# A gated linear recurrence inside a two-layer hybrid decoder: its chunks worked out as a scan

## The chip, the core and the metric

The kernel runs on one core of one Trainium2 chip. TensorE (PE) multiplies, VectorE (DVE) and ScalarE (ACT) do elementwise work and empty PSUM, GpSimd (POOL) does some elementwise work, SyncE (SP) issues most DMAs. The metric is the device time of one execution in microseconds, a median of several runs. Everything is fp32; large products are split into three fp32r products of a high and a low part.

## The reference

A trunk of two layers over 512 tokens of width 1024. Each layer is a feed-forward block, four mixers side by side on a common projection, an output projection, and a second feed-forward block. The change is in one mixer, RWKV-7, with four heads of 64 channels and a 64x64 state S for each head:

```
sa = S @ kk_t
S  = S * w_t - sa (x) (kk_t*a_t) + v_t (x) k_t
y  = S @ r_t
```

It is computed in 8 chunks of 64 tokens; afterwards y is normalized for each head, a bonus is added and a gate multiplied. Another mixer that shares the same stretch of time is NSA, attention with compressed, selected and windowed keys.

## The kernel before

For each mixer pass, 21 projection tiles (tilep, 24 PE products of 512 columns each) make the inputs. Rwkv.prep makes for each head pair j the chunk operands KR (keys kk and queries r, scaled by the running decay), AK (the two kinds of written keys) and W (the chunk's total decay), and puts the transposed v into sav. Rwkv.solve then makes M, the masked products of AK and KR inside each chunk (L1010, masked on DVE at L1012), sends its key part through DRAM (adram) into another layout, inverts 16x16 blocks by forward substitution on DVE (L1030, L1032), sends the result back through DRAM (tdram), and joins the blocks on PE to 64x64 inverses T64 (L1057 to L1088). Last it scales AK by W and transposes it (L1093 to L1097).

Rwkv.chain goes through the chunks in series. For each one: right side from the state H and from v (L898, L901, accumulated in PSUM), copied to R (L904), multiplied by T64 (L910), copied into sav beside v (L911, L912), multiplied by AK (L920), and added to the decayed state (L928 for chunk 0, else four updates at L931). H is kept as five rotating tiles with the two heads of a pair on the diagonal of a 128x128 block. Rwkv.out(g) makes the outputs of four chunks (L948 from the state, L951 from sav), normalizes them (ln, L983 to L995), transposes (L959), gates (L969 to L971) and puts them.

The order of instructions is made ahead of time from priorities: an instruction with a lower number goes first once its operands and buffers are there. Projection tiles 0 to 12 come first. Then solve stands at p0, chain and out at p0 + 300 (chunks 0 to 3) and p0 + 500 (chunks 4 to 7), attention's 16 units at p0 + 2000, and as filler at p0 + 3000 the remaining projection tiles, pool and convolution, with the pool's product at L810. Within an engine the order then is fixed, and an instruction that waits holds up all behind it. PSUM: solve and out take tiles from net.pr (tag "r", two buffers), chain from tag "c" (one). The ring "s" (line 466) has seven SBUF buffers for attention scores, their transposes and the compression weights.

The output projection (order 0, 1, 6, 7, 4, 5, 2, 3 over the mixers' tiles) needs all mixers; 4 and 5 are attention's, 2 and 3 the recurrence's.

Of the kernel before, what the change touches and what calls it, by code (L numbers as in the profile page):

```python
# [26 lines left out]
HD = 64  # L27
C = 64
NC = S // C
# [69 lines left out]
class Net:  # L99
# [290 lines left out]
    def mixers(self, tilep, cmpk, cmpv):  # L390
        nc = self.nc
# [39 lines left out]
        rw = st["rw"]  # L431
# [13 lines left out]
        def chain(g):  # L445
            for _ in rw.chain(g):
                pass
            rw.out(g)
# [17 lines left out]
    def ring(self):  # L466
        return self.mt("s", [P, S], bufs=7)

    def rring(self):
        return self.mt("s", [P, S], F32R, bufs=7)  # L470
# [343 lines left out]
class Rwkv:  # L814
    def __init__(self, net, sh):
        self.net, self.sh = net, sh
        nc = net.nc
        self.T0 = sh["L0"]
        nc.scalar.activation(self.T0, self.T0, AF.Tanh, scale=net.c["sc"])
        nc.vector.tensor_scalar(self.T0[64:], self.T0[64:], 0.5, 0.5, ALU.mult, ALU.add)  # L820
        self.sav = net.mt("sav", [P, NC, 2, 2, HD])
        self.KR, self.AK, self.W, self.bv = [], [], [], []
        self.Hb = []
        for i in range(5):
            h = net.mt(f"H{i}", [P, 2, P])
            nc.gpsimd.memset(h, 0.0)
            self.Hb.append(h)
# [58 lines left out]

    def chain(self, g):
        net = self.net
        nc, sav, KR, W = net.nc, self.sav, self.KR, self.W
        M, T64 = self.M, self.T64  # L890
        for cc in range(4):
            ch = 4 * g + cc
            H = self.Hb[ch % 5]
            pr = net.psum("c", 1)
            for j in range(2):
                a, b = slice(64 * j, 64 * j + 64), slice(64 * (1 - j), 64 * (2 - j))
                if ch > 0:
                    nc.tensor.matmul(pr[a, 0:P], KR[j][:, ch, 0], H[:, j], start=True, stop=False)  # L898
                for hp in range(2):
                    o = pr[a, hp * 64:hp * 64 + 64]  # L900
                    nc.tensor.matmul(o, M[b, j, hp, ch, 0], sav[b, ch, j, hp], start=(ch == 0),  # L901
                                     stop=(ch == 0 or hp == 1))
            R = net.mt("R", [P, P], bufs=2)
            nc.scalar.copy(R, pr[:, :P])  # L904
            pa = net.psum("c", 1)
            for j in range(2):
                a = slice(64 * j, 64 * j + 64)
                for hp in range(2):
                    hs = slice(64 * hp, 64 * hp + 64)
                    nc.tensor.matmul(pa[a, hs], T64[a, hp, ch], R[a, hs], start=True, stop=True)  # L910
            nc.scalar.copy(sav[0:64, ch, 0].rearrange("p b d -> p (b d)"), pa[0:64, :P])  # L911
            nc.vector.tensor_copy(sav[64:, ch, 1].rearrange("p b d -> p (b d)"), pa[64:, :P])  # L912
            if ch == NC - 1:
                yield
                return
            phs = net.psum("c", 1)
            for j in range(2):
                for hp in range(2):
                    hs = slice(64 * hp, 64 * hp + 64)
                    nc.tensor.matmul(phs[hs, j * 64:j * 64 + 64],  # L920
                                     self.AK[j][:, ch].rearrange("p a b -> p (a b)")[:, hs], sav[:, ch, j, hp],
                                     start=True, stop=True)
            Hn = self.Hb[(ch + 1) % 5]
            for hp in range(2):
                hs = slice(64 * hp, 64 * hp + 64)
                p3 = phs[hs, 0:P].rearrange("p (j v) -> p j v", v=HD)
                if ch == 0:
                    nc.vector.tensor_copy(Hn[hs, :, hs], p3)  # L928
                else:
                    for j in range(2):  # L930
                        nc.vector.scalar_tensor_tensor(Hn[hs, j, hs], H[hs, j, hs], W[j][hs, ch:ch + 1],  # L931
                                                       p3[:, j], ALU.mult, ALU.add)
            yield

    def out(self, g):
        net = self.net
        nc, v, sav, KR = net.nc, net.v, self.sav, self.KR
        M = self.M
        py = []
        for j in range(2):  # L940
            p = net.pr()[:, 0:256]
            p4 = p.rearrange("p (c h v) -> p c h v", c=2, h=2)
            for cc in range(4):
                ch = 4 * g + cc
                H = self.Hb[ch % 5]
                par = slice(64 * (ch % 2), 64 * (ch % 2) + 64)
                if ch > 0:
                    nc.tensor.matmul(p4[par, cc // 2].rearrange("p h v -> p (h v)"), KR[j][:, ch, 1], H[:, j],  # L948
                                     start=True, stop=False)
                for hp in range(2):  # L950
                    nc.tensor.matmul(p4[par, cc // 2, hp], M[:, j, hp, ch, 1], sav[:, ch, j, hp], start=(ch == 0),  # L951
                                     stop=(ch == 0 or hp == 1))
# [22 lines left out]
    def ln(self, py):  # L975
        net = self.net
        nc = net.nc
        bc = lambda a: a.unsqueeze(2).to_broadcast([P, 4, HD])
        y = net.tmp()[:, :S].rearrange("p (j c h v) -> p j c h v", j=2, c=2, h=2)
        yf = y.rearrange("p j c h v -> p j (c h) v")  # L980
        mu = net.small(8, "lmu")
        for j in range(2):
            nc.vector.tensor_reduce(mu[:, 4 * j:4 * j + 4], py[j].rearrange("p (a v) -> p a v", v=HD), AX.X, ALU.add)  # L983
        nc.vector.tensor_scalar(mu, mu, 1.0 / HD, None, ALU.mult)
        for j in range(2):
            nc.vector.tensor_sub(yf[:, j], py[j].rearrange("p (a v) -> p a v", v=HD), bc(mu[:, 4 * j:4 * j + 4]))
# [11 lines left out]
    def solve(self):  # L998
        net = self.net
# [20 lines left out]
        dma(blk, ad[:, 0:1024].rearrange("b (i t) -> b i t", t=C)[:, :, 0:16])  # L1020
        Tb = net.tmp()[:, :S].rearrange("p (k a b) -> p k a b", k=2, a=16)
# [67 lines left out]
        for g in range(2):  # L1089
            for j in range(2):  # L1090
                ake = net.tmp()[:, :S].rearrange("p (a b) -> p a b", b=P)
                akv = AK[j][:, 4 * g:4 * g + 4].rearrange("p c a b -> p c (a b)")
                nc.vector.tensor_mul(ake, akv, W[j][:, 4 * g:4 * g + 4].unsqueeze(2).to_broadcast([P, 4, P]))  # L1093
                pk = net.pr()
                for cc in range(4):
                    nc.tensor.transpose(pk[:, cc * P:(cc + 1) * P], ake[:, cc], net.ident)
                nc.scalar.copy(akv, pk.rearrange("p (c a) -> p c a", c=4))  # L1097
        self.M, self.T64 = M, TT

# [125 lines left out]
```

## Time and profile before

| | us |
|---|---|
| median of 3 runs (2081.02 to 2084.48) | 2081.34 |
| the profiled execution | 2080.37 |
| its span, first to last instruction | 2078.6 |
| PE busy | 2026.1 |
| DVE busy | 1042.8 |
| ACT busy | 665.3 |
| POOL busy | 329.9 |

The span is that of the device's instructions; the run's time has 1.8 us around it. Busy times of PE overlap at their ends, as matmuls are pipelined, so the durations of PE's rows can't be added: what an instruction takes of PE's time is read from the start of one row to the start of the next. A row with xN stands for N instructions in series, and each fp32 product counts as two. The two mixing passes lie at about 380 to 660 us and 1410 to 1690 us; the feed-forward blocks, which fill the rest, are PE products without a gap.

### The profile page before, as it was taken

What the parts mean: (1) busy time and instruction counts of PE and PEld (TensorE: products, weight loads), DVE (VectorE), ACT (ScalarE), POOL (GpSimd) and SP (SyncE); (2) the same over time, 40 slices, a digit from 0 to 9 for tenths busy, and PEclk for the clock granted to TensorE, in tenths of its full rate; (3) what the DMA queues carried; (4) which work ended last, traced back from release to release, by engine and by line L of the source; (5) the groups of instructions that cost most, each with busy time, mean ns of one, the idle gap of its engine ahead of it and who ended that gap; (6) DMA issues with size and microseconds to landing.
All of it is one profiled execution on the core that took longest, in us unless ns stands there. A gap on an engine that the chain in (4) does not pass through costs nothing.

```text
span 2078.6 us, 25265 instructions
## 1 busy us (share of the span) xinstructions
PE 2026.1 (97%) x10132; PEld 1646.0 (79%) x10132; DVE 1042.8 (50%) x1866; ACT 665.3 (32%) x1053; POOL 329.9 (16%) x311
## 2 busy tenths in 40 slices
PE   8999999998999999999999999999988999999999
PEld 6888888876767888888888888887766778888887
DVE  5434344567676534343544343355686754334433
ACT  4322223332344322232333222233324443222221
POOL 1110111102332110011011001111033411100110
PEclk9999999998999999999999999999999999999999
DMA  5223223322302322322332232244133032223223
GB/s 198 93 90 103 101 89 124 128 102 64 71 18 91 102 89 82 114 90 89 104 102 102 84 110 100 75 133 149 68 74 77 1 102 102 95 84 116 86 92 97
DMA packets 61078, 196.76 MB, mean 95 GB/s; under 512 B 29472, under 2 KB 29600, under 8 KB 46240
## 3 DMA queue, kind: packets, MB, share of 16 engines
q1 hardware_dynamic: 58400, 186.76, 28.0%
q0 software_dynamic: 2560, 8.39, 1.1%
q8 instruction: 79, 1.29, 0.3%
q14 instruction: 39, 0.32, 0.0%
HBM read 183.58 MB, written 8.93 MB: 93 GB/s over the span
## 4 chain that ended last, share of the span: by engine, by line
PE 92%; DVE 4%; DMA 1%; issue 1%; ACT 1%; POOL 0%; SPq 0%; DVEq 0%; POOLq 0%; ACTq 0%
PE d L209 15%; PE d L210 15%; PE d L211 15%; PE r L211 8%; PE r L209 8%; PE r L210 8%; PE n L209 5%; PE n L211 5%; PE n L210 5%; PE o L623 1%; PE r L1010 1%; PE n L616 1%; PE d L589 0%; PE c L901 0%; DVE t L1032 0%
## 5 line engine op out<-in xcount | busy, mean ns | idle before, releaser
L203 ACT CAST wh<-w 128x1024 fp32r<-128x1024 f32 (+2 forms) x360 | 344.4, 957 | 1103.9 <-issue 334.5
L204 DVE TENSOR_TENSOR wl<-w,wh 128x1024 fp32r<-128x1024 f32 (+2 forms) x360 | 404.4, 1124 | 211.7 <-ACT wh L203 204.1
L209 PE MATMUL d<-hh,wh 128*128 128x512 f32 x1008 | 400.0, 397 | 6.8 <-ACT hh L216 6.8
L210 PE MATMUL d<-hl,wh 128*128 128x512 f32 x1008 | 400.6, 397 | 1.7 <-DVE hl L217 1.7
L211 PE MATMUL d<-hh,wl 128*128 128x512 f32 x1008 | 399.0, 396 | 0.0
L270 POOL TENSOR_TENSOR al<-t,ah 128x512 fp32r<-128x512 f32 x88 | 152.7, 1735 | 1062.5 <-ACT ah L269 1062.5
L210 PE MATMUL r<-hl,wh 128*128 128x512 f32 x736 | 286.8, 390 | 0.0
L211 PE MATMUL r<-hh,wl 128*128 128x512 f32 x736 | 286.5, 389 | 0.0
L209 PE MATMUL r<-hh,wh 128*128 128x512 f32 x736 | 286.5, 389 | 0.0
L209 PEld LDWEIGHTS d<-hh,wh 128*128 128x128 f32 x1008 | 192.6, 191 | 50.2 <-ACT hh L216 6.8
L210 PEld LDWEIGHTS d<-hl,wh 128*128 128x128 f32 x1008 | 192.4, 191 | 44.7 <-DVE hl L217 3.6
L211 PEld LDWEIGHTS d<-hh,wl 128*128 128x128 f32 x1008 | 192.4, 191 | 42.9 <-issue 2.0
L264 DVE TENSOR_TENSOR t<-d,rs 128x512 f32<-128x512 f32 x88 | 60.5, 691 | 266.3 <-PE d L211 260.5
L268 DVE TENSOR_TENSOR t<-t,r 128x512 f32<-128x512 f32 x88 | 60.5, 688 | 221.1 <-PE r L211 220.9
L209 PEld LDWEIGHTS r<-hh,wh 128*128 128x128 f32 x736 | 138.2, 188 | 28.7
L211 PEld LDWEIGHTS r<-hh,wl 128*128 128x128 f32 x736 | 138.2, 188 | 28.6
L210 PEld LDWEIGHTS r<-hl,wh 128*128 128x128 f32 x736 | 138.2, 188 | 28.5
L209 PE MATMUL d<-ah,wh 128*128 128x512 f32 x352 | 136.9, 389 | 0.0
L210 PE MATMUL d<-al,wh 128*128 128x512 f32 x352 | 136.9, 389 | 0.0
L211 PE MATMUL d<-ah,wl 128*128 128x512 f32 x352 | 136.9, 389 | 0.0
L209 PE MATMUL n<-ah,wh 128*128 128x512 f32 x352 | 136.9, 389 | 0.0
L210 PE MATMUL n<-al,wh 128*128 128x512 f32 x352 | 136.9, 389 | 0.0
(307 smaller groups left out, 2372.1 us busy)
## 6 DMA issues: line engine op xcount, KB each, us to landing
w<-in_g SPq DMA_DIRECT2D x87, 1024.0 KB, 4.9
w<-in_d SPq DMA_DIRECT2D x64, 704.0 KB, 4.1
w<-in_win SPq DMA_DIRECT2D x20, 1024.0 KB, 4.9
w<-in_wout SPq DMA_DIRECT2D x8, 1024.0 KB, 5.3
xd<-x POOLq DMA_DIRECT2D x16, 256.0 KB, 4.2
x<-xd POOLq DMA_DIRECT2D x16, 256.0 KB, 5.7
x<-in_x SPq DMA_DIRECT2D x8, 256.0 KB, 5.3
s<-in_cmpk SPq DMA_DIRECT2D x8, 256.0 KB, 5.9
```

What stands on the lines that cost most here:

```text
L203: self.nc.scalar.copy(hi, w)
L204: self.nc.vector.tensor_sub(lo, w, hi.bitcast(F32))
L209: self.nc.tensor.matmul(ps, wh[:, sl], xh[:, k], start=(first and i == 0), stop=False)
L210: self.nc.tensor.matmul(ps, wh[:, sl], xl[:, k], start=False, stop=False)
L211: self.nc.tensor.matmul(ps, wl[:, sl], xh[:, k], start=False, stop=(last and i == n - 1))
L264: nc.vector.tensor_mul(t, pg, self.rs)
L268: nc.vector.tensor_mul(th, th, pu)
L270: nc.gpsimd.tensor_sub(al, th, ah.bitcast(F32))
L616: nc.tensor.transpose(ptr[:, k * P:(k + 1) * P], scs[hp][:, b * P:(b + 1) * P], self.ident)
L623: nc.tensor.matmul(acc, VT[:, br, b], pT[k][:, o:o + 2 * P], start=(br == 0 and b == 0 and k == 0), stop=(br == 1 and b == i and k == 1))
L1010: nc.tensor.matmul(pm[:, i * P:(i + 1) * P], AK[j][hs, ch].rearrange("p a b -> p (a b)"), KR[j][hs, ch].rearrange("p a b -> p (a b)"), sta ...
```

## The change

The serial part of the recurrence is reduced to one product and one addition for each chunk. With G = T64 times the transposed keys, a chunk maps the state as H' = W*H + (AK^T G) H + AK^T u, where u = T64 M v needs no state. All G and u are worked out for all chunks together (carry, called at the end of solve), and from them the transition matrices (put into KR's key part) and the effective queries (added to KR's query part, as r + M G). What doesn't need the inverses (the transposed keys KT, the products of M and v, the scaled and transposed AK) is worked out in early, called in solve between the sending of M to DRAM and the forward substitution. out then takes the state against the effective queries, with K of 64 for each head in place of the block diagonal of 128; ln follows the new layout. The five H tiles (and their memsets) become one, and the ring "s" goes from seven buffers to six.

```diff
-        return self.mt("s", [P, S], bufs=7)
+        return self.mt("s", [P, S], bufs=6)
 ...
+    def early(self, M):
 ...
+        for g in range(2):
+            pk, pm = net.pr(), net.pr()
+            for j in range(2):
+                a, b = slice(64 * j, 64 * j + 64), slice(64 * (1 - j), 64 * (2 - j))
+                for cc in range(4):
+                    ch = 4 * g + cc
+                    nc.tensor.matmul(pk[a, cc * P:(cc + 1) * P], KR[j][:, ch, 0], net.ident, start=True, stop=True)
+                    for hp in range(2):
+                        o = cc * P + hp * HD
+                        nc.tensor.matmul(pm[a, o:o + HD], M[b, j, hp, ch, 0], sav[b, ch, j, hp], start=True, stop=True)
+            nc.scalar.copy(self.KT[:, 4 * g:4 * g + 4].rearrange("p c h k -> p (c h k)"), pk)
+            self.take(g, pm)
 ...
+    def carry(self):
 ...
+        for g in range(2):
+            pg, pu = net.pr(), net.pr()
+            for j, cc, hp, ch, a in each(g):
+                o = cc * P + hp * HD
+                nc.tensor.matmul(pg[a, o:o + HD], T64[a, hp, ch], self.KT[a, ch, hp], start=True, stop=True)
+            for j, cc, hp, ch, a in each(g):
+                o = cc * P + hp * HD
+                nc.tensor.matmul(pu[a, o:o + HD], T64[a, hp, ch], sav[a, ch, j, hp], start=True, stop=True)
+            for j, copy in enumerate((nc.scalar.copy, nc.vector.tensor_copy)):
+                a = slice(64 * j, 64 * j + 64)
+                copy(M[a, j, :, 4 * g:4 * g + 4, 0], pg[a].rearrange("p (c h k) -> p h c k", c=4, h=2))
+            self.take(g, pu)
+        for g in range(2):
+            pp = [net.pr(), net.pr()]
+            for j, cc, hp, ch, a in each(g):
+                hs, o = slice(64 * hp, 64 * hp + 64), cc * HD
+                nc.tensor.matmul(pp[j][hs, o:o + HD], M[a, j, hp, ch, 0],
+                                 AK[j][a, ch].rearrange("p a b -> p (a b)")[:, hs], start=True, stop=True)
+            for j, cc, hp, ch, a in each(g):
+                hs, o = slice(64 * hp, 64 * hp + 64), 256 + cc * HD
+                nc.tensor.matmul(pp[j][hs, o:o + HD], M[a, j, hp, ch, 0], M[a, j, hp, ch, 1], start=True, stop=True)
+            for j in range(2):
 ...
+                nc.scalar.copy(KR[j][:, cs, 0], part(0))
+                nc.vector.tensor_add(KR[j][:, cs, 1], KR[j][:, cs, 1], part(256))
 ...
     def chain(self, g):
+        for ch in range(4 * g, min(4 * g + 4, NC - 1)):
+            p = net.psum("c", 1)
             for j in range(2):
+                o = slice(j * HD, j * HD + HD)
                 for hp in range(2):
                     hs = slice(64 * hp, 64 * hp + 64)
+                    nc.tensor.matmul(p[hs, o], AK[j][:, ch].rearrange("p a b -> p (a b)")[:, hs], sav[:, ch, j, hp],
+                                     start=True, stop=(ch == 0))
+                if ch > 0:
+                    for hp in range(2):
+                        hs = slice(64 * hp, 64 * hp + 64)
+                        nc.tensor.matmul(p[hs, o], KR[j][hs, ch, 0], H[hs, ch, j], start=False, stop=True)
+            if ch == 0:
+                nc.vector.tensor_copy(H[:, 1].rearrange("p j v -> p (j v)"), p[:, 0:P])
+            else:
+                for j in range(2):
+                    nc.vector.scalar_tensor_tensor(H[:, ch + 1, j], H[:, ch, j], W[j][:, ch:ch + 1],
+                                                   p[:, j * HD:j * HD + HD], ALU.mult, ALU.add)
 
     def out(self, g):
 ...
+        for hp in range(2):
+            hs = slice(64 * hp, 64 * hp + 64)
+            p = net.pr()[:, 0:256].rearrange("p (j c v) -> p j c v", j=2, c=2)
+            for j in range(2):
+                for cc in range(4):
+                    ch = 4 * g + cc
+                    o = p[64 * (ch % 2):64 * (ch % 2) + 64, j, cc // 2]
+                    nc.tensor.matmul(o, M[:, j, hp, ch, 1], sav[:, ch, j, hp], start=True, stop=(ch == 0))
+                    if ch > 0:
+                        nc.tensor.matmul(o, KR[j][hs, ch, 1], self.H[hs, ch, j], start=False, stop=True)
             py.append(p)
 ...
     def solve(self):
 ...
         dma(blk, ad[:, 0:1024].rearrange("b (i t) -> b i t", t=C)[:, :, 0:16])
+        self.early(M)
         Tb = net.tmp()[:, :S].rearrange("p (k a b) -> p k a b", k=2, a=16)
 ...
-        for g in range(2):
-            for j in range(2):
-                ake = net.tmp()[:, :S].rearrange("p (a b) -> p a b", b=P)
 ...
         self.M, self.T64 = M, TT
+        self.carry()
```

early also holds the loop over AK that stood at the end of solve, and take copies one half of a PSUM tile into sav on ACT and the other on DVE.

## Rows read from the trace of the kernel before

**Rows 1.** the page, busy time of TensorE and the chain that ended last
```profile
PE 2026.1 (97%) x10132; PEld 1646.0 (79%) x10132; DVE 1042.8 (50%) x1866; ACT 665.3 (32%) x1053; POOL 329.9 (16%) x311
...
PE 92%; DVE 4%; DMA 1%; issue 1%; ACT 1%; POOL 0%; SPq 0%; DVEq 0%; POOLq 0%; ACTq 0%
```

**Rows 2.** busy time by stage, layer 0: PE, PEld, DVE, ACT, POOL, then PEclk
```profile
480.00:505.00 25.00, 25.00 (x154) 20.18 (x153) 19.47 (x36) 9.09 (x15) 3.44 (x7) 1.00 0.43 122
505.00:515.00 10.00, 2.61 (x6) 1.11 (x5) 8.93 (x20) 1.22 (x2) 6.81 (x7) 0.71 0.13 13
515.00:545.00 30.00, 28.03 (x222) 22.15 (x220) 19.64 (x60) 7.70 (x19) 11.83 (x12) 0.87 0.53 114
...
631.00:660.00 29.00, 25.19 (x122) 19.43 (x121) 17.89 (x46) 13.03 (x26) 7.51 (x10) 1.00 0.37 120
sum 180.00, PE 160.52 PEld 123.24 DVE 127.63 ACT 72.45 POOL 58.94; mean PE 20.07 PEld 15.40 DVE 15.95 ACT 9.06 POOL 7.37
```

**Rows 3.** the same table for the mixing pass of layer 1, its sum
```profile
sum 180.00, PE 160.27 PEld 122.35 DVE 130.54 ACT 73.44 POOL 60.92; mean PE 20.03 PEld 15.29 DVE 16.32 ACT 9.18 POOL 7.62
```

**Rows 4.** list of waits, engine PE: us in total, times, longest
```profile
PE n L810 <- DVE t L1032: 14.8, 2, 7.4
...
PE c L898 <- DVE H L931: 2.4, 3, 1.3
```

**Rows 5.** timeline of PE at the long wait: start us, us, instruction
```profile
505.26 0.39 PE L210 MATMUL d<-hl,wh 128*128 128x512 f32 x1
505.48 0.39 PE L211 MATMUL d<-hh,wl 128*128 128x512 f32 x1
513.26 2.05 PE L810 MATMUL n<-u,mat 128*128 128x512 f32 x2 [7.39 <-DVE t L1032]
...
516.17 0.63 PE L211 MATMUL d<-hh,wl 128*128 128x512 f32 x1
516.60 0.63 PE L209 MATMUL d<-hh,wh 128*128 128x512 f32 x1
```

**Rows 6.** timeline of PE, one chunk of the recurrence, layer 0
```profile
587.07 0.43 PE L898 MATMUL c<-H,KR 128*64 128x128 f32 x2
587.43 0.44 PE L901 MATMUL c<-sav,M 64*64 64x64 f32 x4
587.81 0.43 PE L898 MATMUL c<-H,KR 128*64 128x128 f32 x2
...
590.68 0.46 PE L910 MATMUL c<-R,TT 64*64 64x64 f32 x8
591.06 0.33 PE L616 MATMUL n<-cst,s 128*128 128x128 f32 x1
...
621.63 0.32 PE L898 MATMUL c<-H,KR 128*64 128x128 f32 x1
```

**Rows 7.** timeline of PE, products of 128 columns, layer 0
```profile
479.69 1.71 PE L1010 MATMUL r<-KR,AK 64*128 64x128 f32 x16
481.33 0.32 PE L901 MATMUL c<-sav,M 64*64 64x64 f32 x2
```

**Rows 8.** timeline of PE, a block of 32 instructions, layer 0
```profile
547.32 1.15 PE L1071 MATMUL r<-TT,t 64*64 64x64 f32 x32
548.40 0.39 PE L623 MATMUL o<-s,VT 128*128 128x256 f32 x1
```

**Rows 9.** timeline of PE, layer 1: old output products, first, and behind the last
```profile
1650.76 0.39 PE L948 MATMUL r<-H,KR 128*64 128x128 f32 x2
...
1652.85 0.63 PE L623 MATMUL o<-s,VT 128*128 128x256 f32 x3
```

**Rows 10.** groups by line, 380 to 720 us: busy us, mean ns, idle before
```profile
L931 DVE SCALAR_TENSOR_TENSOR H<-H,W,c 64x64 f32<-64x64 f32 x24 | 5.8, 277 | 0.2
...
L1093 DVE TENSOR_TENSOR t<-AK,W 128x512 f32<-128x512 f32 x4 | 2.7, 688 | 3.2 <-PE r L1057 3.2
```

**Rows 11.** list of waits, SP's queue: us in total, times, longest
```profile
SPq L679 <- PE n L682: 9.2, 2, 4.7
```

More of the change, by code (lines that the diff above doesn't have):

```diff
@@ L445, in chain @@
         def chain(g):
-            for _ in rw.chain(g):
-                pass
+            rw.chain(g)
             rw.out(g)
@@ L822, in __init__ @@
         self.KR, self.AK, self.W, self.bv = [], [], [], []
[L823 to L827, printed above, removed]
+        self.H = net.mt("H", [P, NC, 2, HD])
     def prep(self, j):
@@ new lines, in take @@
+    def take(self, g, ps):
+        nc, sav = self.net.nc, self.sav
+        for j, copy in enumerate((nc.scalar.copy, nc.vector.tensor_copy)):
+            a = slice(64 * j, 64 * j + 64)
+            copy(sav[a, 4 * g:4 * g + 4, j].rearrange("p c h v -> p c (h v)"), ps[a].rearrange("p (c x) -> p c x", c=4))
+    def carry(self):
+        net = self.net
+        nc, sav, KR, AK, M, T64 = net.nc, self.sav, self.KR, self.AK, self.M, self.T64
+        each = lambda g: [(j, cc, hp, 4 * g + cc, slice(64 * j, 64 * j + 64)) for cc in range(4) for j in range(2)
+                          for hp in range(2)]
+        for g in range(2):
[6 more added lines that the diff above has]
+                nc.tensor.matmul(pu[a, o:o + HD], T64[a, hp, ch], sav[a, ch, j, hp], start=True, stop=True)
+            for j, copy in enumerate((nc.scalar.copy, nc.vector.tensor_copy)):
+                a = slice(64 * j, 64 * j + 64)
+                copy(M[a, j, :, 4 * g:4 * g + 4, 0], pg[a].rearrange("p (c h k) -> p h c k", c=4, h=2))
+            self.take(g, pu)
+        for g in range(2):
+            pp = [net.pr(), net.pr()]
[7 more added lines that the diff above has]
+            for j in range(2):
+                part = lambda o: pp[j][:, o:o + 256].rearrange("p (c k) -> p c k", c=4)
+                cs = slice(4 * g, 4 * g + 4)
+                nc.scalar.copy(KR[j][:, cs, 0], part(0))
+                nc.vector.tensor_add(KR[j][:, cs, 1], KR[j][:, cs, 1], part(256))
@@ L887, in chain @@
     def chain(self, g):
         net = self.net
[L889 to L894, printed above, removed]
-            for j in range(2):
[L896 to L905, printed above, removed]
-            for j in range(2):
-                a = slice(64 * j, 64 * j + 64)
+        nc, sav, KR, AK, W, H = net.nc, self.sav, self.KR, self.AK, self.W, self.H
@@ L913, in chain @@
[L913 to L932, printed above, removed]
@@ L939, in out @@
         py = []
[L940 to L952, printed above, removed]
+        for hp in range(2):
+            hs = slice(64 * hp, 64 * hp + 64)
+            p = net.pr()[:, 0:256].rearrange("p (j c v) -> p j c v", j=2, c=2)
+            for j in range(2):
+                for cc in range(4):
+                    ch = 4 * g + cc
[3 more added lines that the diff above has]
+                        nc.tensor.matmul(o, KR[j][hs, ch, 1], self.H[hs, ch, j], start=False, stop=True)
             py.append(p)
@@ L977, in ln @@
         nc = net.nc
[L978 removed]
         y = net.tmp()[:, :S].rearrange("p (j c h v) -> p j c h v", j=2, c=2, h=2)
[L980 removed]
         mu = net.small(8, "lmu")
[L982 to L983 removed]
+        m4 = mu.rearrange("p (j c h) -> p j c h", j=2, c=2)
+        for hp in range(2):
+            nc.vector.tensor_reduce(m4[:, :, :, hp], py[hp], AX.X, ALU.add)
         nc.vector.tensor_scalar(mu, mu, 1.0 / HD, None, ALU.mult)
[L985 to L986 removed]
+        for hp in range(2):
+            nc.vector.tensor_sub(y[:, :, :, hp], py[hp], m4[:, :, :, hp].unsqueeze(3).to_broadcast([P, 2, 2, HD]))
         t = net.tmp()[:, :S]
```

22 lines of the change are left out of this document (10 added, 12 removed).

## The prediction

> **What bounds the kernel now.** I read the page's engine totals first: TensorE (PE) is busy 2026.1 us, 97% of the span, and the chain that ended last lies on PE for 92% of it [rows 1]. So a microsecond of PE work added anywhere costs about a microsecond, unless it lands where PE stands still; a shorter dependency chain pays only where PE waits for it. Then the table by stages of the two mixing passes, the only places that the change touches: in the 180 us from 480 to 660 us PE is busy 160.5 us, in the same stretch of layer 1 160.3 us [rows 2, 3]. So 19.5 us and 19.7 us of PE idle time are all that can be won, plus what the lowered clock costs (granted clock 0.71 and 0.87 in two of the stages shown [rows 2]). Then the list of PE's waits: the longest is 7.4 us, once in each layer, at the pool mixer's product L810, behind the forward substitution L1032 on VectorE (DVE); the state H of the recurrence, which the change is about, holds PE up 2.4 us in three waits over both layers [rows 4]. Last the timeline of PE at the 7.4 us wait: the products of 512 columns before it follow each other at 0.22 us, those behind it at 0.43 us [rows 5], nine of them, which are the clock's two levels, 2.4 and 1.2 GHz, after the engine had stood still.
>
> Thus the recurrence is long (its chunks begin 8.6 us apart: five starts of L898 from 587.07 to 621.63 us [rows 6]), but attention (NSA) fills PE meanwhile. A shorter series is worth little by itself; what counts is how much PE work replaces it and whether the new work falls into the idle time.
>
> **Prices.** All at full clock, from one layer, start to next start. Sixteen instructions of 128 columns take 1.64 us, 0.103 us each [rows 7] (each fp32 product is two instructions). In the old chain, two of these on 128x64 weights (L898) take 0.36 us and four of 64 columns on 64x64 weights (L901) 0.38 us, alternating [rows 6]. Two times 0.103 is 0.205, so a change of weight shape costs 0.155 us, and one 64-column instruction (0.38 - 0.155)/4 = 0.056 us. Eight that lie on different quarters of the array (L910) take 0.38 us [rows 6], so 0.028 us each behind the change. Thirty-two (L1071) take 1.08 us with the change behind them [rows 8].
>
> **Removed, for each layer.** Seven chunks with a state part, 2 x (0.36 + 0.38) = 1.48 us each: 10.4. Chunk 0's two groups of L901: 0.8. Eight L910 groups at 0.38: 3.0. Seven L920 groups (also eight instructions) at 0.38: 2.7. The old out: 36 instructions of one shape take 2.09 us in the densest stretch, from 1650.76 to 1652.85 us [rows 9], 0.058 us each; 92 of them 5.3, with eight changes of shape 6.5. Together 23.4 us of PE time. The scaling and transposing of AK (L1093 to L1097) only moves forward.
>
> **Added, for each layer.** early: 16 products of 128 columns with the identity (32 x 0.103 = 3.3) and 32 of 64 columns (64 x 0.056 = 3.6). They are written in turn, but the PSUM buffer of the first kind comes free one mask product earlier, so I expect runs, four changes of shape: 7.5 us; 11.8 if they alternate, 32 changes. carry: 128 products, eight blocks as in [rows 8]: 8.6 us; 9.9 if attention cuts each block once. chain: six chunks of four groups (AK, KR, AK, KR), four instructions each, 4 x 0.028 + 0.155 = 0.27 us a group, and chunk 0: 6.8 us; 5.0 if both AK groups go together. out: the products of M with sav (K of 128) and of KR with H (now K of 64) have different shapes, where before all were 128x64. For the first half the M products are ready long before the state and go in runs: 56 x 0.056 plus four changes, 3.7 us. For the second half its PSUM buffers come only after the first half's normalization, when all states exist, so the written order holds and shapes alternate: 32 groups of 2 x 0.056 + 0.155 = 0.267, 8.5 us. Together 12.2 (7.8 with two runs, 16.0 with both alternating). Sum 35.1 us, bounds 28.9 and 44.5. **Net PE work: +11.7 us a layer, bounds +5.5 and +21.1.**
>
> The rows show that a change of weight shape costs 0.155 us [rows 6]. The Trainium skill (TensorEngine Tiling (Array Packing), Key Properties) has this as a rule that speaks against the change: "Changing tiling mode (not just tile) drains the TensorE". The trace agrees. With the changes free on both sides (74 added, 53 removed) the net would be +8.4 instead of +11.7.
>
> **Other engines.** DVE loses 34 instructions, 24 of them state updates of 0.277 us [rows 10], and gains 23 of two to four times the width (12 updates, one copy, ten copies and additions in early and carry); I set this against each other. The four scalings of AK now stand ahead of the substitution on DVE, in the wait for the round trip through DRAM; if that cover is too short they delay the solve by at most their 2.7 us [rows 10], in which PE still has projection tiles. The five memsets on GpSimd that go were off the path.
> The ring of score and weight buffers loses one of seven. On SP's queue the loads of the compression weights wait already for PE's reads, 9.2 us in two waits, the longest 4.7 us [rows 11], and behind them stand the projection weights. No row prices one buffer less: between nothing and half the longest wait, 2.35 us a layer. I take 0.5, nearer to nothing, since PE is busy 25.00 of 25 us ahead of the gap [rows 2].
>
> **What is won, for each layer.** The 7.4 us wait: early's products need neither substitution nor pool, they precede both in the written order and outrank the filler, so 7.5 us of PE work lies where PE stood still; as DVE also starts a little later, I leave 2 us: -5.4. The slow products behind it: nine at 0.21 us too much are 1.9; -1.4. Idle time of 515 to 545 us (1.97 us [rows 2]): half, since filler pushed back by early is still there; -1.0. The chain's own waits (1.2 us a layer from H, a little from its other two hops): seven hops instead of 23; -0.8. End, 631 to 660 us, 3.8 us idle [rows 2], in part for the last out: it now ends before attention; -1.5. Together -10.1, bounds -3.3 (wait and clock as before) and -15.3 (7.4 and 1.9 in full, 2.0, 1.2 and 2.8 of the others).
>
> **Sum.** +11.7 + 0.5 - 10.1 = +2.1 us a layer, +4.2 in all. The profiled execution took 2080.4 us (1.8 around its span), 1.0 under the median 2081.3. So 2084.6 by it, and **2085 us** as a median.
>
> **The rivals.**
> Stalls go, faster. The chain needs one PE and one DVE step per chunk: four groups and two updates, about 1.08 + 0.55 us and some 1 us of queueing, 2.7 instead of 8.6 us. If out comes in runs (+11.7 - 4.4 = +7.3) and all of the 15.3 us is won, it is -8.0 a layer: 2065 us. For it: the long wait lies just where early is written. Against: PE is 97% busy already.
> Shapes alternate, slower. If early and both halves of out follow the written order, the bound of +21.1 holds: +21.1 + 0.5 - 10.1 = +11.5 a layer, 2104 us. It decides from the point where a layer has some 65 changes of shape (10.1/0.155) more than now. For it: the old chain shows strict alternation in the written order [rows 6]. Against: the old out shows long runs where buffers allow [rows 9]. The tiling page's rule is this mechanism.
> The long wait stays, slower. PE's order is fixed beforehand; if L810 is again put ahead of filler and behind early, PE stands as long, merely later: +11.7 + 0.5 - 3.3 = +8.9 a layer, 2099 us. For it: two waits of the same length, 14.8 us in sum [rows 4]; the late start of the substitution on DVE isn't touched.
> The series isn't shorter. If each state update queues behind attention's work on DVE, a chunk still takes some 8 us; the chain's and the end's 2.3 us are not won, +4.4 a layer: 2090 us. Against: the updates have the higher priority.
>
> **How the numbers follow.** About balanced, as summed: 0.40; its own range is 2076 to 2094, up by early alternating (2 x 4.3 us), down by the rest of the long wait and as much again of the others (2 x 4.5 us). Stalls go 0.26, alternation 0.14, the wait stays 0.15, no shorter series 0.05. A measurement of this kernel tells a change from none from about 0.2%, 4.2 us. Below 2077: 0.26 and 0.06 of the balanced case, 0.32. Within 4.2 us: 0.22, all from the balanced case. Above: the rest of it (0.12) and the slow rivals (0.34), 0.46. The range 2065 to 2105 leaves out what goes beyond the fast and the alternating rival.
>
> **What the changed profile would show.** PE instructions up by about 540 (272 a layer) in a span that ends within 20 us of before; early's products between 495 and 515 us, with L810's wait below 3 us; shapes in runs in early and in alternation in the second half of out, groups of two some 0.27 us apart; chunk starts 2.5 to 3.5 us apart from about 572 us on; attention, not the recurrence, as the last thing ahead of the output projection. The forecast is wrong if the net PE time of the named lines isn't +8 to +15 us a layer, if L810 waits as before, or if PE idles over 8 us behind the chain's end, when attention runs alone.

## The result, and the profile after

The changed kernel takes 2110.14 us (median of 4 runs, 2106.22 to 2111.72) where the kernel before took 2081.18 us beside it: a ratio of 1.0138, 95% interval 1.0113 to 1.0164. It is 1.4% slower. The forecast was 2085 us with a range to 2105, so the time lies outside. The profiled execution took 2109.03 us, its span is 2107.2 us.

The page of the changed kernel, the lines that answer to [rows 1]: PE has 544 instructions more (about 540 were expected), 35.7 us more busy time, and carries still more of the chain that ended last.

```profile
PE 2061.8 (98%) x10676; PEld 1680.7 (80%) x10676; DVE 1043.5 (50%) x1844; ACT 669.1 (32%) x1045; POOL 330.5 (16%) x301
...
PE 94%; DVE 4%; ACT 1%; issue 1%; DMA 0%; POOL 0%; SPq 0%; DVEq 0%; ACTq 0%
```

To compare whole mixing passes I cut each from the first product of its normalization (L250) to that of the next feed-forward layer. One row is one pass: window, its length, then busy time of PE, PEld, DVE, ACT and POOL, then PE's granted clock. First the kernel before, layer 0 and layer 1:

```profile
392.26:706.35 314.09, 294.61 (x1881) 229.01 (x1880) 209.01 (x530) 120.42 (x252) 74.16 (x82) 0.94 0.25 75
1425.94:1733.39 307.45, 287.72 (x1882) 222.98 (x1880) 208.00 (x530) 120.28 (x252) 73.01 (x82) 0.97 0.25 75
```

Then the changed kernel:

```profile
392.18:715.78 323.60, 308.83 (x2154) 243.39 (x2152) 208.98 (x519) 121.89 (x248) 75.71 (x82) 0.93 0.25 73
1435.37:1762.00 326.63, 310.04 (x2154) 243.72 (x2153) 209.33 (x519) 122.60 (x248) 74.75 (x82) 0.93 0.24 71
```

So the passes are 9.5 and 19.2 us longer, 28.7 together, which is the whole difference. PE's busy time grew by 14.2 and 22.3 us; its idle time (length less busy) fell from 19.5 and 19.7 to 14.8 and 16.6, by 4.7 and 3.1. DVE's work is unchanged, as forecast. More PE work and a lower clock, not more idle time, made the kernel slower. By the trace's record of the clock, PE stood at the lower of its two levels for 95 us of the two passes, before for 58.

Where in layer 0: the table by stages of the kernel before, two stages that [rows 2] does not show,

```profile
590.00:610.00 20.00, 17.78 (x142) 13.35 (x142) 16.66 (x67) 9.88 (x30) 6.30 (x6) 0.91 0.00 1
610.00:631.00 21.00, 20.31 (x173) 15.44 (x171) 16.95 (x55) 10.96 (x29) 10.82 (x7) 1.00 0.00 1
```

and the changed kernel, with the stages that answer to [rows 2] too:

```profile
505.00:515.00 10.00, 10.00 (x79) 8.11 (x79) 5.23 (x10) 3.97 (x8) 1.36 (x2) 1.00 0.15 15
515.00:545.00 30.00, 24.54 (x137) 19.37 (x136) 22.69 (x83) 11.79 (x33) 14.22 (x15) 0.88 0.55 114
...
590.00:610.00 20.00, 19.88 (x138) 14.73 (x138) 8.41 (x36) 3.77 (x11) 3.42 (x3) 0.66 0.00 1
610.00:631.00 21.00, 19.64 (x112) 14.64 (x112) 12.42 (x43) 7.28 (x20) 5.93 (x5) 0.81 0.00 1
```

Two things are to be seen. The stage from 505 to 515 us, in which PE was busy 2.61 us [rows 2], is full, at a granted clock of 1.00: early's products fill the long wait as forecast. But the next stage gives about half of it back (24.54 us busy where it was 28.03). And from 590 to 631 us PE is busy nearly all the time at a granted clock of 0.66 and 0.81 while DVE, with 16.66 us of work in the first of these stages before, now finds 8.41.

What lies there is out(). The timeline of PE in the changed kernel (start us, us, instruction), first half of out and the chain's products ahead of it and in it:

```profile
585.33 0.34 PE L955 MATMUL c<-sav,AK 128*64 128x64 f32 x4 [1.25 <-DVE H L965]
...
588.41 0.34 PE L980 MATMUL r<-sav,M 128*64 128x64 f32 x4
588.68 0.32 PE L982 MATMUL r<-H,KR 64*64 64x64 f32 x2
588.93 0.33 PE L980 MATMUL r<-sav,M 128*64 128x64 f32 x2
589.19 0.33 PE L982 MATMUL r<-H,KR 64*64 64x64 f32 x2
...
589.97 0.34 PE L955 MATMUL c<-sav,AK 128*64 128x64 f32 x4
590.23 0.33 PE L960 MATMUL c<-H,KR 64*64 64x64 f32 x4
...
592.39 0.47 PE L982 MATMUL r<-H,KR 64*64 64x64 f32 x2
...
595.21 0.48 PE L980 MATMUL r<-sav,M 128*64 128x64 f32 x4
595.62 0.47 PE L982 MATMUL r<-H,KR 64*64 64x64 f32 x2
```

The shapes alternate, one product (two instructions) at a time; a group takes 0.26 us from start to start, and from 592.39 us on 0.40 us. That is the second of the clock's two levels (1.2 instead of 2.4 GHz), and the engine fell to it in the middle of this alternation, without any idle time since 585.33 us. In layer 1 it also falls inside both halves of out, at 1629.8 and 1657.1 us.

The groups of instructions on those two lines (busy us, mean ns), same pass, with two of the largest groups of attention; before, L623 (now L622) had 19.2 us at 340 ns. The spans of alternating lines overlap at their ends, so 11.0 and 11.0 can't be added; from start to start the two lines took 18.1 us.

```profile
L622 PE MATMUL o<-s,VT 128*128 128x256 f32 x80 | 21.3, 370 | 3.5 <-DVE s L618 1.9 <-DVE T L633 0.8 <-ACT s L617 0.7
L615 PE MATMUL n<-cst,s 128*128 128x128 f32 x80 | 15.4, 309 | 1.6 <-POOL s L597 1.6
L982 PE MATMUL r<-H,KR 64*64 64x64 f32 x56 | 11.0, 287 | 0.0
L980 PE MATMUL r<-sav,M 128*64 128x64 f32 x64 | 11.0, 286 | 0.0
```

And the list of PE's waits over the whole span (us, times, longest), beside [rows 4]: the pool product's 14.8 us are gone from it. Attention's own waits have come up in their place, behind two waits of the projections.

```profile
...
PE n L615 <- POOL s L597: 3.9, 3, 1.6
PE o L622 <- DVE s L618: 3.5, 7, 1.0
PE o L622 <- ACT s L617: 3.0, 7, 0.6
PE d L588 <- DVE mx L590: 2.6, 5, 0.9
```

### The profile page after: what moved, and what is told of

Same layout as the page of the kernel before. It is cut to its first block, busy times and chain, and to the rows that moved or that the text cites. A ratio compares the mean times of both kernels' runs of the same rounds, so it can differ in the third digit from the quotient of the medians.

```text
span 2107.2 us, 26337 instructions
## 1 busy us (share of the span) xinstructions
PE 2061.8 (98%) x10676; PEld 1680.7 (80%) x10676; DVE 1043.5 (50%) x1844; ACT 669.1 (32%) x1045; POOL 330.5 (16%) x301
## 4 chain that ended last, share of the span: by engine, by line
PE 94%; DVE 4%; ACT 1%; issue 1%; DMA 0%; POOL 0%; SPq 0%; DVEq 0%; ACTq 0%
PE d L209 15%; PE d L210 15%; PE d L211 15%; PE r L211 8%; PE r L209 8%; PE r L210 8%; PE n L209 4%; PE n L211 4%; PE n L210 4%; PE o L622 1%; PE r L982 1%; PE r L980 1%; PE n L615 1%; PE r L1039 1%; PE d L588 1%
## 5 line engine op out<-in xcount | busy, mean ns | idle before, releaser
L211 PE MATMUL n<-ah,wl 128*128 128x512 f32 x352 | 137.1, 389 | 0.0
```

Of the source, the lines that this page charges most:

```text
L211: self.nc.tensor.matmul(ps, wl[:, sl], xh[:, k], start=False, stop=(last and i == n - 1))
```

## The experiments

Theory A: the alternation of weight shapes in out() is the mis-sized term. It costs PE time itself, and the granted clock falls in it, which slows the attention products that run beside and behind it. Rivals: B, attention waits because the recurrence's products are done before it; C, the smaller ring of buffers makes attention wait; and for early's place, that it is worth its 5.4 us a layer or that it is not. Each ratio below is against the kernel before, run beside it on the same chip; times of different runs were partly taken on different chips.

### Out in runs

All of a half's and head's M products go first, then all KR products.

```diff
-            for j in range(2):
-                for cc in range(4):
 ...
-                    nc.tensor.matmul(o, M[:, j, hp, ch, 1], sav[:, ch, j, hp], start=True, stop=(ch == 0))
-                    if ch > 0:
-                        nc.tensor.matmul(o, KR[j][hs, ch, 1], self.H[hs, ch, j], start=False, stop=True)
+            for i, (j, ch, o) in enumerate(each):
+                nc.tensor.matmul(o, M[:, j, hp, ch, 1], sav[:, ch, j, hp], start=(i < 2), stop=False)
+            for i, (j, ch, o) in enumerate(each):
+                if ch > 0:
+                    nc.tensor.matmul(o, KR[j][hs, ch, 1], self.H[hs, ch, j], start=False, stop=(i > 5))
```

> The changed kernel, only out() written otherwise: for each half and head first the eight products of M with sav (128x64 weights), then the eight of KR with H (64x64 weights), so that a group of products has one shape. The changed kernel took 2110 us. Theory A (the changes of weight shape in out are the mis-sized term, and they slow the clock under the attention products beside them): out's 120 instructions cost 120 x 0.056 + 8 x 0.155 = 8 us a layer instead of 18.1 and 18.4, so about 20 us less in all, 2090 us; and if the granted clock of the stages 590 to 631 us (0.66 and 0.81) rises to those of before (0.91 and 1.00), up to 10 us more, 2080 us. Rival B (attention, left alone behind the shorter recurrence, is what waits): PE gets shorter work but stands idle for it, PE's idle time rises by most of the 10 us a layer, 2103 to 2110 us.

Measured: 2074.66 us, ratio 0.9972 [0.9959, 0.9985], so 35 us below the changed kernel, and faster than the kernel before. The groups of out() in this kernel, layer 0 (busy us, mean ns)

```profile
L978 PE MATMUL r<-sav,M 128*64 128x64 f32 x64 | 2.7, 228 | 0.0
L981 PE MATMUL r<-H,KR 64*64 64x64 f32 x56 | 2.7, 225 | 0.0
```

and its stages from 590 to 631 us, columns as above:

```profile
590.00:610.00 20.00, 18.48 (x199) 13.97 (x198) 16.76 (x66) 9.45 (x27) 7.69 (x6) 1.00 0.01 2
610.00:631.00 21.00, 17.99 (x145) 13.33 (x141) 20.13 (x67) 12.39 (x32) 11.66 (x8) 1.00 0.08 25
```

The two lines fall from 18.1 to 4.8 us from start to start, the clock is 1.00 in both stages, DVE has its work again. Its two mixing passes:

```profile
392.12:699.63 307.51, 291.55 (x2153) 230.75 (x2152) 208.71 (x519) 121.82 (x248) 75.76 (x82) 0.96 0.25 76
1419.22:1726.93 307.71, 292.31 (x2153) 231.02 (x2152) 207.70 (x519) 122.30 (x248) 75.11 (x82) 0.96 0.25 75
```

PE's busy time is 17.3 and 17.7 us below the changed kernel; its idle time is 16.0 and 15.4. Even theory A's larger gain (to 2080 us) was too small: 8 us were expected for out, at 0.056 us an instruction, and its 120 instructions took 4.8, 0.040 us each. Rival B's gain eaten by idle time did not come. What this run cannot tell is whether runs helped by shape or by bringing M's products forward.

### One shape, in the written order

H keeps zeros in its off-diagonal blocks, so KR with H can use all 128 rows, like M with sav. Out's written order stays.

```diff
-                        nc.tensor.matmul(o, KR[j][hs, ch, 1], self.H[hs, ch, j], start=False, stop=True)
+                        nc.tensor.matmul(o, KR[j][:, ch, 1], self.H[:, ch, j, hs], start=False, stop=True)
```

> The changed kernel with out() in its written order (M with sav, KR with H, in turn), but H kept with zeros in the off-diagonal blocks, as before the change, so that KR with H has 128x64 weights like M with sav: the same instructions of PE in the same order, one shape. The state updates are four a chunk instead of two. Theory A (the change of shape is the cost): out costs 120 x 0.056 us and some ends, about 8 us a layer as in the kernel with runs, and the stage from 590 to 631 us keeps a granted clock of 1.00: within 6 us of that kernel's 2075 us. Rival (runs helped because M's products went early and out became shorter in series): out stays at 14 us a layer or more, 2095 us or more.

Measured: 2068.08 us, ratio 0.9945 [0.9931, 0.996]: by the ratios (1.0138 less 0.9945, of 2081 us) 40 us below the changed kernel. No kernel here is faster beyond its interval. Timeline of PE in this kernel, out's first half and the chain beside it:

```profile
590.08 0.34 PE L954 MATMUL c<-sav,AK 128*64 128x64 f32 x4
590.35 0.33 PE L959 MATMUL c<-KT,KR 64*64 64x64 f32 x4
590.61 0.33 PE L981 MATMUL r<-sav,M 128*64 128x64 f32 x2
590.78 0.28 PE L983 MATMUL r<-KT,KR 128*64 128x64 f32 x2
590.89 0.33 PE L981 MATMUL r<-sav,M 128*64 128x64 f32 x4
591.01 0.28 PE L983 MATMUL r<-KT,KR 128*64 128x64 f32 x2
```

(KT is the buffer in which H now lies.) The chain still changes shape and takes 0.26 us a group; out's groups, in turn as written, start 0.11 to 0.17 us apart. Its groups of out(), layer 0

```profile
L981 PE MATMUL r<-sav,M 128*64 128x64 f32 x64 | 4.3, 230 | 0.0
L983 PE MATMUL r<-KT,KR 128*64 128x64 f32 x56 | 4.1, 222 | 0.0
```

and its stages from 590 to 631 us, columns as above:

```profile
590.00:610.00 20.00, 17.39 (x154) 13.29 (x152) 18.41 (x72) 8.76 (x24) 8.34 (x7) 1.00 0.01 2
610.00:631.00 21.00, 19.15 (x162) 15.00 (x161) 19.42 (x66) 12.30 (x31) 11.70 (x7) 1.00 0.08 25
```

So it is the change of shape, not the place of M's products: with as many products in nearly the same order, and 13 DVE instructions more a layer, the cost and the low clock go. The zeros cost nothing that can be seen: from start to start out takes 4.5 and 4.9 us in the two layers, in runs of two shapes 4.8 and 5.0, one by one 18.1 and 18.4. The Trainium skill says that a change of tiling mode drains the engine (TensorEngine Tiling (Array Packing), Key Properties); the trace agrees, at 0.26 us a group against 0.11 to 0.17.

### Out in pairs

Two M products, two KR products, in turn.

```diff
+                    for ch, o in two:
+                        nc.tensor.matmul(o, M[:, j, hp, ch, 1], sav[:, ch, j, hp], start=True, stop=(ch == 0))
+                    for ch, o in two:
+                        if ch > 0:
+                            nc.tensor.matmul(o, KR[j][hs, ch, 1], self.H[hs, ch, j], start=False, stop=True)
```

> The changed kernel with out() in pairs: two products of M with sav, two of KR with H, in turn; half as many changes of shape. Theory A, by dose: out is 120 x 0.056 + 32 x 0.155 = 11.7 us a layer at full clock, where one by one gave 18.2 and runs gave 8.2; the time lies between 2075 and 2110, about in proportion at 2088 us. Rival (only the order of M ahead of H counts): as the changed kernel, 2105 to 2110 us.

Measured: 2088.49 us, ratio 1.0039 [1.0024, 1.0054]. With half as many changes the time comes out as expected. From start to start out's two lines take 10.0 and 9.0 us, between 18.1 and 4.8, and the clock lies between as well. The groups in this kernel

```profile
L983 PE MATMUL r<-H,KR 64*64 64x64 f32 x56 | 6.2, 263 | 0.0
L980 PE MATMUL r<-sav,M 128*64 128x64 f32 x64 | 6.1, 264 | 0.0
```

and its stages from 590 to 631 us, columns as above:

```profile
590.00:610.00 20.00, 18.86 (x147) 13.77 (x147) 10.99 (x47) 5.47 (x15) 5.74 (x5) 0.74 0.00 1
610.00:631.00 21.00, 18.67 (x138) 14.14 (x139) 18.06 (x62) 10.05 (x25) 9.78 (x7) 0.92 0.00 1
```

### The chain in runs too

```diff
-            for j in range(2):
-                o = slice(j * HD, j * HD + HD)
 ...
+            for j, o, hs, hp in each:
+                nc.tensor.matmul(p[hs, o], AK[j][:, ch].rearrange("p a b -> p (a b)")[:, hs], sav[:, ch, j, hp],
+                                 start=(j == 0), stop=(ch == 0 and j == 1))
+            if ch > 0:
+                for j, o, hs, hp in each:
+                    nc.tensor.matmul(p[hs, o], KR[j][hs, ch, 0], H[hs, ch, j], start=False, stop=(j == 1))
```

> As the kernel with out() in runs, and in each chunk of the chain both AK products first, then both KR products: two groups instead of four. Theory A: twelve changes of shape fewer a layer, 12 x 0.155 = 1.9 us, 3.7 us in all below the kernel with only out() in runs. Rival: the second group of KR waits for the second state update, the AK group of the next chunk no longer fills that wait, and a chunk of the chain takes no less; within 2 us of that kernel.

Measured: 2080.55 us, ratio 1.000 [0.9991, 1.001]: 6 us above the kernel with only out in runs, where 3.7 below was expected. The rival said "within 2 us", so neither hit. The chain itself did fall, from 4.4 + 4.0 to 3.2 + 3.1 us of busy time on its two lines in layer 0 (6.2 to 4.9 from start to start). But the passes' busy time rose, to 294.38 and 293.89 us, and the idle time to 17.3 and 17.5. The clock, 1.00 in the stages from 590 to 631 us with only out in runs, is 0.91 and 0.84 here. So runs in out alone do not hold the clock at 1.00: PE stood idle for some 3 us of each of these two stages, in the changed kernel for 0.1 and 1.4. Why the order that came out is worse I did not settle.

### One shape in the chain too

```diff
-                        nc.tensor.matmul(p[hs, o], KR[j][hs, ch, 0], H[hs, ch, j, hs], start=False, stop=True)
+                        nc.tensor.matmul(p[hs, o], KR[j][:, ch, 0], H[:, ch, j, hs], start=False, stop=True)
```

> The kernel with one shape in out(), and in the chain too: KR with H on 128x64 weights like AK with sav, so that a chunk's four groups have one shape, in the written order. Theory A: 24 changes of shape a layer fewer (24 x 0.155 = 3.7 us) against 24 products that no longer overlap (48 instructions x 0.028 = 1.3 us): 2.4 us a layer, 4.8 us below the one-shape kernel's 2068, 2063 us, and the chain's occupied time falls from 6.6 to about 4.3 us a layer. Rival (in the chain PE waits for the state update anyway, as in the kernel with the chain in runs, which was 6 us slower): within 3 us of 2068 or above.

Measured: 2069.06 us, ratio 0.9939 [0.9918, 0.9961]; not to be told from the one-shape kernel. The chain is cheaper, and PE then waits for the state; its two groups here, where the one-shape kernel had 4.5 and 4.0 us with 1.0 us of idle time:

```profile
L954 PE MATMUL c<-sav,AK 128*64 128x64 f32 x56 | 3.9, 234 | 1.9 <-DVE KT L966 1.6 <-DVE KT L963 0.2
L959 PE MATMUL c<-KT,KR 128*64 128x64 f32 x48 | 3.2, 224 | 0.0
```

The rival's figure holds, its mechanism in layer 0 alone: there PE's busy time is 1.4 us shorter than with one shape in out only, and its idle time 1.6 us longer. In layer 1 the pass is 4.2 us longer, at a granted clock of 0.96 instead of 0.98; why, no run shows.

### Early moved behind the substitution

```diff
-        self.early(M)
         Tb = net.tmp()[:, :S].rearrange("p (k a b) -> p k a b", k=2, a=16)
 ...
+        self.early(M)
         self.carry()
```

> The changed kernel, only the call of early() moved from ahead of the forward substitution to just ahead of carry(). If early's products (6.7 us of PE a layer) are what took the place of the 7.4 us wait at the pool product, the wait comes back in both layers and the products stand in series behind it: 10 to 15 us more than the changed kernel, 2120 to 2125 us. Rival: early's place is worth nothing, because the order of PE around the substitution is chosen anew and other ready work (filler, attention) takes the gap: within 4 us of 2110.

Measured: 2102.75 us, ratio 1.0108 [1.0093, 1.0123]: by the ratios 6 us faster than the changed kernel, with intervals that overlap, where 10 to 15 us slower was expected and within 4 us by the rival. The expectation missed; the rival is not ruled out. The wait at the pool product did come back, 15.9 us in two waits. The clock in the stage from 590 to 610 us was 0.83 instead of 0.66 and from 610 to 631 us 1.00 instead of 0.81, so the move is mixed with the alternation. Hence the same move in the kernel with out in runs:

> The kernel with out() in runs, with the call of early() moved to just ahead of carry(). With the shapes alternating this move made the kernel 7 us faster although the wait at the pool product came back. Theory A (that was the slower clock under attention, moved about; what fills the pool product's wait is given back in attention's own waits): within 5 us of 2075. Rival (with out mended, early's place ahead of the substitution is worth the 5.4 us a layer of the prediction): 2083 to 2090 us.

Measured: 2073.68 us, ratio 0.9968 [0.9951, 0.9985]; out in runs with early in its place had 0.9972. The first line of PE's waits in this kernel

```profile
PE n L809 <- DVE t L1060: 16.0, 2, 8.1
```

and its two mixing passes:

```profile
392.24:701.69 309.45, 290.98 (x2154) 229.60 (x2153) 207.34 (x519) 122.44 (x248) 73.14 (x82) 0.96 0.25 76
1421.27:1729.23 307.96, 290.94 (x2153) 231.74 (x2152) 208.89 (x519) 122.12 (x248) 74.00 (x82) 0.94 0.25 75
```

Two waits of 8 us are back, yet PE's idle time is only 2.5 and 1.6 us longer (18.5 and 17.0 instead of 16.0 and 15.4), its busy time 0.6 and 1.4 us shorter. Filling the long wait was worth about 1.9 us and 0.3 us a pass in these executions, not 5.4, and nothing that the medians can tell. With the wait, attention's products find their inputs ready; without it they wait for them: the idle time before attention's four lines of products (L588, L615, L622, L626) is 5.2 and 2.3 us a pass with early moved, 8.1 and 9.4 with early in its place, 3.8 and 3.2 in the kernel before. That the other engines use PE's pause to get ahead would explain it; it is argued, not shown.

### The chain's priority number raised

The chain and out get the number 1000 instead of 300 (out in runs). Attention has 2000 and the lower number goes first, so this does not put them behind attention, as the expectation has it; it puts them behind more of solve.

```diff
-    PRI = (0, 0, 300, 2000, 3000)
+    PRI = (0, 0, 1000, 2000, 3000)
```

> The kernel with out() in runs, and the chain and out with a lower priority than attention (offset 1000 instead of 300). Theory B (attention waits more because the recurrence's products, which used to lie between its own, are done before it): the idle time of PE at attention's value products (9.6 and 10.1 us a layer) falls towards the 2.9 and 5.1 us of the kernel before, 2065 us. Rival (these waits come from attention's own steps on the other engines, whatever lies beside them, or the recurrence now ends last): no gain, 2075 to 2085 us.

Measured: 2075.48 us, ratio 0.9976 [0.9964, 0.9987]. No gain; idle time 14.9 and 15.4 us. carry ends earlier (its last addition in layer 0 at 581.75 instead of 588.44 us), but the chain lies among attention's products as before: in layer 0 its last chunk starts at 596.8 us (599.9 with 300), and attention's last value product at 638.6 (638.3). So this run does not test theory B. What speaks against B is the run with out in runs, where no idle time ate the gain; that attention's new waits come from the recurrence being done sooner stays open.

### The ring alone

The kernel before with six score and weight buffers instead of seven:

```diff
-        return self.mt("s", [P, S], bufs=7)
+        return self.mt("s", [P, S], bufs=6)
 ...
-        return self.mt("s", [P, S], F32R, bufs=7)
+        return self.mt("s", [P, S], F32R, bufs=6)
```

> The kernel before, only its ring of score and weight buffers with six instead of seven. Prediction: 0.5 us a layer, 2082 us. Rival C (the waits of attention that are new in the changed kernel, +3 to +4.4 us a layer, come from the smaller ring): 2087 to 2092 us.

Measured: 2072.47 us, ratio 0.9963 [0.9948, 0.9978]. One buffer fewer makes the kernel before 8 us faster. Its two passes:

```profile
391.93:709.27 317.34, 296.54 (x1881) 229.93 (x1880) 208.08 (x530) 120.16 (x252) 74.45 (x82) 0.94 0.24 74
1428.86:1729.26 300.40, 284.32 (x1882) 221.76 (x1880) 207.28 (x530) 120.78 (x252) 71.97 (x82) 0.98 0.25 77
```

Layer 0 loses 3.2 us, layer 1 wins 7.1, and there the pool product waits no longer: one wait of 7.4 us is left in the list instead of two. That fits a ring that acts by the order in which PE's instructions come and not by a price for each wait, but no run shows it by itself. And out in runs with seven buffers again:

> The kernel with out() in runs, with seven score and weight buffers as before the change (the states take the place of the transposed keys, which are dead by then). Rival C (the ring of six is what lengthens attention's waits): the idle time at attention's value products (9.6 and 10.1 us a layer) falls by 3 us or more and the time to 2068 us. Theory A (the ring is no term): within 4 us of 2075, and the idle time stays.

Measured: 2081.73 us, ratio 1.0008 [0.9998, 1.0019], 7 us above the same kernel with six; its passes have 17.8 and 18.2 us of idle time. Before the value products (L622) alone PE's idle time is shorter, 2.8 and 4.1 us where six buffers gave 4.9 and 5.2, but the kernel isn't faster. Theory C falls as an account of the time, with its sign reversed: in both pairs of runs six buffers are faster. (Here the states lie in the buffer of the transposed keys, which could have a part in it; the one-shape kernel has them there as well and is the fastest.) The stages from 590 to 631 us of this kernel, with out in runs:

```profile
590.00:610.00 20.00, 17.90 (x152) 13.39 (x150) 16.06 (x64) 10.19 (x28) 7.43 (x6) 0.83 0.00 1
610.00:631.00 21.00, 18.97 (x88) 13.80 (x89) 17.91 (x64) 11.97 (x31) 10.57 (x7) 0.84 0.07 25
```

## Why the prediction was wrong

Point by point, a layer; PE time here is from start to start, as in the prediction, layer 0 and layer 1. The kernel became 28.7 us longer where 4.2 were forecast. Of the 24.5 us between, 7.7 are PE work on the recurrence's lines, 9.6 idle time that was not won and 8.2 the rest of PE's busy time, attention's above all, less the 1.0 that was forecast for the ring.

- **PE bounds, and a shorter series by itself is worth little.** Right. The chain's starts now lie between 574.4 and 607.6 us, and the kernel is slower.
- **early, +7.5.** Right: 6.7 and 6.7. Its products came in runs of 16 and 32 instructions.
- **carry, +8.6.** Right: 8.7 and 9.5.
- **chain, +6.8.** Nearly: 7.6 and 8.0, part of it at the lower clock. The chunks did not come 2.5 to 3.5 us apart: in DVE's timeline of layer 0 the state updates start at 575.91, 584.71, 586.63, 591.14, 601.47 and 606.10 us, the longest stretch across out's alternating products.
- **Removed, 23.4.** Low: 27.0 and 25.5 by the same count of the trace of before.
- **out, +12.2.** This is the term of the PE work that failed: 18.1 and 18.4, above even the bound of 16.0. The step was "for the first half the M products are ready long before the state and go in runs". They were ready, but out's turn comes only behind the chain's first three chunks: its first half starts at 588.41 us, and the third state update, the last that it needs, starts at 586.63 and takes 0.47 us. Nor had the M products a place before: out takes its PSUM from the two buffers that carry uses too, and the first of these came free at 586.38 us, at the end of carry's addition. Which of the two held them no run separates. With all inputs there, the written order holds, and both halves alternate. The price of a group was right (0.267 against 0.26 us), its parts were not: an instruction in runs takes 0.040 and not 0.056 us, so a change costs some 0.18 and not 0.155. What the term lacked besides is the clock: at 0.40 us a group half of out costs half as much again.
- **The clock.** Not in the sum at all. The prediction priced all added work at full speed and looked at the clock only behind the long wait. In layer 0 attention's three largest lines took 54.3 us of busy time (21.3, 17.6 and 15.4) where one shape in out gave 50.3 (19.4, 16.9 and 14.0) and the kernel before 50.0. Over both passes PE stood at the lower level for 95 us, with pairs 68, in runs 51, with one shape 34, in the kernel before 58. Of those 37 us more than before, a third to a half is lost (a group of out takes 0.40 instead of 0.26 us, a product of 512 columns 0.43 instead of 0.22): an estimate of 13 to 18 of the 28.7 us.
- **Net PE work, +11.7 (bounds +5.5 and +21.1).** Measured on the recurrence's lines: +14.0 and +17.1, inside the bounds, though the second is outside the +8 to +15 that the prediction set itself as a sign. Attention's four lines of products grew by 3.7 and 6.9 us, and the projections shrank by 2.3 and 1.4.
- **The long wait, -5.4, and the other idle time, -3.3.** This term failed too. The wait went, as said. But idle time fell by 4.7 and 3.1 us in all, not 8.7; with out mended, the runs show early's place worth 1.9 us and 0.3, and idle time 3.5 and 4.3 us below the kernel before. The prediction did not ask what PE would wait for next; it was attention's own steps. The slow products behind the wait (-1.4) did go: that is the 2.3 and 1.4 us of the projections.
- **Ring, +0.5.** Wrong in sign in the two kernels that were run with six and with seven: 7 to 8 us of the whole kernel in favour of six.
- **The rivals.** The one on alternating shapes came nearest, at a chance of 0.14: both halves of out did alternate, early did not. It asked for some 65 changes of shape a layer more than before. Counted in the traces, PE changes its weight shape 179 and 175 times a pass, before 158 and 163 times, so with 21 and 12 more the kernel is slower than that rival's 2104 us. It too left out the clock and booked the idle time as won.

What the change does when this is mended: the one-shape kernel, at 0.9945 [0.9931, 0.996], beats both kernels. But the kernel before with six buffers has 0.9963 [0.9948, 0.9978], and these intervals overlap: of the gain, the scan's own part cannot be told from none. With seven buffers on both sides, out in runs has 1.0008, no gain either. Why six buffers give the better order, and whether another order would give back what early fills, stays open.

## What to carry to other kernels

When products of two weight shapes are to run in turn, count the changes in the order that the instructions will really have (which inputs are ready when the group's turn comes, not when each input is ready), and either group them or give the smaller product the larger one's shape by zeros; this was worth 35 to 40 us here. Price the stretch, not only the instructions: in every kernel here whose out alternated the granted clock fell in the middle of that stretch, and attention's products beside and behind it ran slower too. And before booking a long wait as won, find the next input that PE will wait for: filling 16 us of waits gave about 2 us in the profiled executions, and nothing in the medians.

## What the runs showed of the hardware

- The granted clock fell in a stretch where the profile shows PE as busy without a gap. By doses, 590 to 610 us of layer 0: 0.66 with shapes changing at every product, 0.74 at every second, 1.00 in runs and 1.00 with one shape. Two other kernels with out in runs had 0.83 (seven buffers) and 0.91 (the chain in runs too) there, but with 2.1 and 3.2 us of idle time in the stage. Nor are changes of shape all that such a fall can follow: with out in runs the clock fell at 471.2 us as well, shortly behind 24 instructions of two columns each (L504, 2.6 us from start to start), and PE was busy for all of the 7 us from 464 to 471; in the changed kernel the same stretch stayed at 1.00. In the changed kernel, from 590 to 600 us, PE is busy all of 10 us at 0.61, most of it thus at the lower level, while DVE finds 2.28 us of work:

```profile
590.00:600.00 10.00, 10.00 (x67) 7.05 (x66) 2.28 (x8) 0.63 (x1) 1.08 (x1) 0.61 0.01 2
```

- A group between two changes of shape takes 0.26 us whether it holds two instructions of 64 columns (L982) or four (L960), at full clock; at half clock 0.40. Two more instructions in such a group cost nothing here.
- The same kernel, with one buffer fewer in a ring that PE's inputs and outputs pass through, took 8 us less (and 7 us less with out in runs).
